# A transformer layer's matmul kernel: fixed order up to LayerNorm 1, one first group of two features, and the first half of gate and up in written order

## The chip, the core and the metric

The kernel runs on one core of a Trainium2 chip, as one launch. A core has engines that run side by side, each with its own queue of instructions: PE (TensorE, matmuls), ACT (ScalarE), DVE (VectorE), POOL (GpSimd) and SP (SyncE, which here issues most DMAs). They meet through semaphores. Matmuls read SBUF and write to PSUM banks. The metric is the time of one execution in device microseconds (us).

## The reference, cut to what matters

One layer over 256 latent tokens and 256 context tokens, D = 2048, all in fp32:

```python
sh1, sc1, g1, sh2, sc2, g2 = ada_mods(c, w_ada, b_ada)      # silu(c) @ w_ada + b_ada, six parts of D
csh1, csc1, *_ = ada_mods(c_ctx, w_ada, b_ada)
q, k, v of x   from modulate(x, sh1, sc1) @ w_in            # 2048 x 3072
q, k, v of ctx from modulate(ctx, csh1, csc1) @ w_in
heads = concat(window_sink_attention(...), global_attention(...))
x = layer_norm(ALPHA * x + g1 * (heads @ w_out))            # LayerNorm 1
u = modulate(x, sh2, sc2)
h = silu(u @ w_gate) * (u @ w_up)                           # 2048 x 5632 each
x = layer_norm(ALPHA * x + g2 * (h @ w_down))
```

## The kernel before

Each fp32 product is made as three products of rounded operands: a value is split into `hi` (rounded to fp32r, by a cast on ACT) and `lo` (the rest, by a subtraction on DVE), and a product of two values is hi·hi + lo·hi + hi·lo (`mm3`, L334 to L337: three matmuls of 128 x 128 by 128 x 512). Weights come in loads of 1 MB as a rule (`raw`, four buffers, L267), and are split in pieces of 1024 columns into `hi` and `lo` tiles (four buffers each, L268).

**Up to LayerNorm 1** the work is a list of steps with an engine, a length, what they wait for and which buffers they take and give (`Flow`, `F.add`). `F.run` (L229, called at L1522) plans an order when the kernel is built: it plays the steps forward with the given lengths, plays them backward for due times, and tries 1400 random changes of the ranks. Then it emits the steps in the best order found. PE also has 56 fill steps (`WARM`, L1354, the matmuls of L1343), which the plan may put wherever PE would wait. The input features of `x @ w_in` (16 blocks of 128) come in groups, `GROUPS` (L41): 1, 1, 2, 4 and 8 features. For each group the modulation is first made from columns of `w_ada` (L654, matmuls of the conditioning vector with loaded weights, or on DVE for the last four features), then `x` is flipped, modulated and split, and then multiplied with the group's rows of `w_in`, block by block. For the very first group the columns of `x` are loaded at once at L379 to L381.

All of this stands in a region (`tc.manual_schedule`, L369, with all five engines) in which each engine issues its instructions in the order in which the code emits them. The region goes on behind `F.run`, over the modulated operand of the next stage (`u2h`, `u2l`, L1676 to L1686), the first four products of gate and up, written out by hand, their copies to SBUF (L1715), and the normalisation of the other columns. It ends at L1719.

**The first half of gate and up** stands behind that end, so that its order is the scheduler's of the framework: it may take a later instruction of an engine ahead of an earlier one where data allow. It computes, for the first ten blocks `f` of 512 columns, the part of the sums over the first features: the first 4 of 16 feature blocks for `f` below 3, the first 8 for the others (`groups`, L1657), and for gate (`i` = 0) and up (`i` = 1). A step (L1664) is one load of weights for four feature blocks, with `project` (L1561): load on SP, then for each of two pieces a cast on ACT (L325) and a subtraction on DVE (L326), then 24 matmuls on PE. Where a sum has all its steps, its two row tiles are copied from PSUM to SBUF by ACT (`spill`, L1670):

```python
def step(g, f=f, i=i, w_=w_, st=st):
    if g == 0:
        st["accs"] = [acc_bank() for _ in range(NT)]
    project(st["accs"], w_, f, g, 0, groups[f] * 4 - 1)
    if g == groups[f] - 1:
        for t in range(NT):
            nc.scalar.copy(spills[f][i][:, t, :], st["accs"][t])
```

The list `first_half` holds these steps in order: two for f = 0 (made by hand ahead, so not run again), four for f = 1 and 2, and 28 for f = 3 to 9. Between them stand side sums: `scales` and `side` make the rest of the modulation from `w_ada` on DVE (L454, a load and two to four multiply-adds each), with a transpose and a sum on DVE (L1193, L1194), a fold on PE (L769) and small steps on DVE and POOL. `z_part(kk)` (L1538) makes two feature blocks of the operand: flips on PE (L1542), two activations and a cast on ACT (L1546, L1548), a subtraction on DVE (L1549).

**The second half** of gate and up (L1774) is again a region with all engines in written order; there a sum's ACT and DVE work is written two and more steps later than its last product. Then comes `w_down`, under the scheduler, and a tail on DVE and ACT.

Of the kernel before, what the change touches and what calls it, by code (L numbers as in the profile page):

```python
# [23 lines left out]
P = 128  # L24
# [16 lines left out]
GROUPS = ((0, 1), (1, 1), (2, 2), (4, 4), (8, 8))  # L41
# [6 lines left out]
WARM = 56  # L48
VECTOR_K = (12,)
EARLY_WARM = 5  # L50
COLD = 3
SEED = 4
# [13 lines left out]
SEED_G = 3  # L66
# [3 lines left out]
GET_NS = 1300  # L70

# [11 lines left out]
class Flow:  # L83

    ENGINES = ("SP", "PE", "ACT", "DVE", "POOL")
    SAME = {"SP": 0, "PE": 0, "ACT": 120, "DVE": 80, "POOL": 80}
    OTHER = {"SP": 2000, "PE": 270, "ACT": 180, "DVE": 160, "POOL": 150}  # L90
    AGAIN = 1300
    ROUNDS = 8
    TRIES = 1400
    DRAWS = 4
    LATE = {"SP": 1000.0, "ACT": 100.0, "DVE": 100.0}

    def __init__(self, room, begin):
        self.room, self.begin, self.steps, self.at = dict(room), begin, [], 0.0

    def add(self, eng, ns, fn, after=(), take=(), give=(), at=None, since=0.0):  # L100
        s = Step()
        s.since = since
        s.eng, s.ns, s.fn, s.take, s.give = eng, ns, fn, take, give
        s.after = [a if isinstance(a, tuple) else (a, 0) for a in after if a is not None]
        s.rank = (self.at if at is None else at, len(self.steps))
        for b in give:
            b.left += 1
        self.steps.append(s)
        return s

    def lag(self, a, b):
        return (self.SAME if a.eng == b.eng else self.OTHER)[a.eng]

    def forward(self):

        room, free, back, order, now = dict(self.room), dict(self.begin), [], [], 0.0
        later, ready = ({e: [] for e in self.ENGINES} for _ in range(2))
        left = {b: b.left for s in self.steps for b in s.give}
        for s in self.steps:
            s.next, s.left, s.when = [], len(s.after), s.since  # L120
        for s in self.steps:
            for a, early in s.after:
                a.next.append((s, early))
            if not s.left:
                heapq.heappush(later[s.eng], (s.when, s.rank, s))
        while len(order) < len(self.steps):
            while back and back[0][0] <= now:
                room[heapq.heappop(back)[1]] += 1
            moved = False
            for e in self.ENGINES:  # L130
                while later[e] and later[e][0][0] <= now:
                    heapq.heappush(ready[e], heapq.heappop(later[e])[1:])
                if free[e] > now:
                    continue
                for item in sorted(ready[e]):
                    s = item[1]
                    pools = [next((p for p in b.pools if room[p] > 0), None) for b in s.take]
                    if None in pools or any(room[p] < pools.count(p) for p in pools):
                        continue
                    ready[e].remove(item)  # L140
                    heapq.heapify(ready[e])
                    for b, p in zip(s.take, pools):
                        b.pool = p
                        room[p] -= 1
                    s.start, free[e] = now, now + s.ns
                    for b in s.give:
                        left[b] -= 1
                        if left[b] == 0:
                            lag = self.AGAIN if b.loaded else self.OTHER[e]
                            heapq.heappush(back, (free[e] + lag, b.pool))  # L150
                    for n, early in s.next:
                        n.left -= 1
                        n.when = max(n.when, free[e] - early + self.lag(s, n))
                        if n.left == 0:
                            heapq.heappush(later[n.eng], (n.when, n.rank, n))
                    order.append(s)
                    moved = True
                    break
            if not moved:
                times = [free[e] for e in self.ENGINES if free[e] > now and (ready[e] or later[e])]  # L160
                times += [later[e][0][0] for e in self.ENGINES if later[e] and later[e][0][0] > now]
                times += [back[0][0]] if back else []
                if not times:
                    return None, None
                now = min(times)
        return order, max(s.start + s.ns for s in self.steps)

    def backward(self, end):

        free = {e: end for e in self.ENGINES}  # L170
        later, ready = ({e: [] for e in self.ENGINES} for _ in range(2))
        left, by, start, now = {s: len(s.next) for s in self.steps}, {s: end for s in self.steps}, {}, end
        for s in self.steps:
            if not left[s]:
                heapq.heappush(later[s.eng], (-end, -(s.start + s.ns), s.rank, s))
        while len(start) < len(self.steps):
            moved = False
            for e in self.ENGINES:
                while later[e] and -later[e][0][0] >= now:
                    heapq.heappush(ready[e], heapq.heappop(later[e])[1:])  # L180
                if free[e] < now or not ready[e]:
                    continue
                s = heapq.heappop(ready[e])[-1]
                start[s] = free[e] = now - s.ns
                moved = True
                for a, early in s.after:
                    left[a] -= 1
                    by[a] = min(by[a], start[s] + early - self.lag(a, s))
                    if left[a] == 0:
                        heapq.heappush(later[a.eng], (-by[a], -(a.start + a.ns), a.rank, a))  # L190
            if not moved:
                times = [free[e] for e in self.ENGINES if free[e] < now and (ready[e] or later[e])]
                now = max(times + [-later[e][0][0] for e in self.ENGINES if later[e] and -later[e][0][0] < now])
        return start

    def replay(self, order, draw):

        free, rooms, end, late = dict(self.begin), {p: [0.0] * n for p, n in self.room.items()}, {}, {}
        left = {b: b.left for s in self.steps for b in s.give}
        for s, pools in order:  # L200
            t = max(free[s.eng], s.since, *(end[a] - early + self.lag(a, s) for a, early in s.after), 0.0)
            for b, p in zip(s.take, pools):
                t = max(t, heapq.heappop(rooms[p]))
                b.pool = p
            free[s.eng] = t + s.ns
            end[s] = free[s.eng] + draw.random() * (self.LATE.get(s.eng, 0.0) if s.ns else 0.0)
            for b in s.give:
                left[b] -= 1
                late[b] = max(late.get(b, 0.0), end[s] + (self.AGAIN if b.loaded else self.OTHER[s.eng]))
                if left[b] == 0:  # L210
                    heapq.heappush(rooms[b.pool], late[b])
        return max(end.values())

    def plan(self):
        order, last = self.forward()
        if not order:
            return False
        order = [(s, [b.pool for b in s.take]) for s in order]
        end = sum(self.replay(order, random.Random(i)) for i in range(self.DRAWS)) / self.DRAWS
        if end > self.end:  # L220
            return False
        self.end, self.last, self.rank, self.best = end, last, [s.rank[0] for s in self.steps], order
        return True

    def give_ranks(self, ranks):
        for i, (s, r) in enumerate(zip(self.steps, ranks)):
            s.rank = (r, i)

    def run(self):  # L229
        self.best, self.end = None, math.inf  # L230
        for _ in range(self.ROUNDS):
            self.plan()
            order, last = self.forward()
            if not order:
                break
            late = self.backward(last)
            self.give_ranks([late[s] for s in self.steps])
        assert self.best, "no step can start"
        draw = random.Random(SEED)
        for _ in range(self.TRIES):  # L240
            ranks = list(self.rank)
# [10 lines left out]
        for s, pools in self.best:  # L252
            for b, b.pool in zip(s.take, pools):
                pass
# [1718 lines left out]
```

## Time and profile before

| | us |
|---|---|
| median of 3 runs | 1124.76 (1124.49 to 1125.29) |
| profiled execution, span | 1124.1 |
| PE busy in it | 1103.7 |
| DVE busy | 905.7 |
| ACT busy | 603.6 |
| first product of `w_in` starts at | 16.4 |
| first half of gate and up, from its first product | 388.8 to 583.5 |
| last matmul starts at | 1111.6 |

A line of a timeline gives start, length, engine, line of the kernel, operation, the tiles (out<-in), shapes, a count, and in brackets the idle time of the engine before it with what ended it. A line of the view by window gives the stretch, its length, then busy time and instructions of PE, PEld (weight load), DVE, ACT and POOL, the granted clock of PE (1.00 is full), the DMA share and GB/s; asked for one line of code, it gives PE and PEld alone. A line of the view of waits says who waited for whom: us in total, times, longest. A line of the chain gives start, length and what ran. Matmul rows last longer than their distance (0.39 us against 0.23), since they are pipelined.

### The profile page before, as it was taken

What the parts mean: (1) busy time and instruction counts of PE and PEld (TensorE: products, weight loads), DVE (VectorE), ACT (ScalarE), POOL (GpSimd) and SP (SyncE); (2) the same over time, 40 slices, a digit from 0 to 9 for tenths busy, and PEclk for the clock granted to TensorE, in tenths of its full rate; (3) what the DMA queues carried; (4) which work ended last, traced back from release to release, by engine and by line L of the source; (5) the groups of instructions that cost most, each with busy time, mean ns of one, the idle gap of its engine ahead of it and who ended that gap; (6) DMA issues with size and microseconds to landing.
All of it is one profiled execution on the core that took longest, in us unless ns stands there. A gap on an engine that the chain in (4) does not pass through costs nothing.

```text
span 1124.1 us, 14152 instructions
## 1 busy us (share of the span) xinstructions
PE 1103.7 (98%) x5241; PEld 893.4 (79%) x5241; DVE 905.7 (81%) x1097; ACT 603.6 (54%) x879; POOL 47.1 (4%) x86
## 2 busy tenths in 40 slices
PE   8999999999999999999999999999999999999995
PEld 7677788788888778888888888888888788888884
DVE  3758999999989988787756876887875899678886
ACT  3335584787684355544464555655554565345541
POOL 1000050101200011000000000000000000000000
PEclk9999999999999999999999999999999999999998
DMA  9999999697999879989858798998896576546651
GB/s 298 388 391 373 390 366 370 225 312 215 356 311 375 303 284 341 326 309 340 295 189 297 264 340 273 314 308 302 311 321 222 159 253 223 190 149 231 225 217 75
DMA packets 179452, 321.27 MB, mean 286 GB/s; under 512 B 8979, under 2 KB 51379, under 8 KB 177077
## 3 DMA queue, kind: packets, MB, share of 16 engines
q1 hardware_dynamic: 177350, 319.23, 81.1%
q10 hardware_dynamic: 1808, 1.11, 0.3%
q8 instruction: 41, 0.67, 0.2%
q14 instruction: 29, 0.24, 0.1%
q0 software_dynamic: 224, 0.02, 0.0%
HBM read 304.07 MB, written 16.25 MB: 285 GB/s over the span
## 4 chain that ended last, share of the span: by engine, by line
PE 94%; DVE 3%; DMA 2%; issue 0%; ACT 0%; DVEq 0%; ACTq 0%
PE acc L335 22%; PE acc L336 22%; PE acc L337 22%; PE wk L337 7%; PE wk L336 7%; PE wk L335 7%; PE wk L1130 2%; PE wk L654 2%; PE wk L1343 1%; DMA raw<-in_w_in_dram 1%; PE wk L822 1%; DMA raw<-in_w_ada_dram 1%; DMA adav<-in_b_ada_dram 1%; DVE adav L454 0%; DVE lo L332 0%
## 5 line engine op out<-in xcount | busy, mean ns | idle before, releaser
L326 DVE TENSOR_TENSOR lo<-raw,hi 128x1024 fp32r<-128x1024 f32 x232 | 280.5, 1221 | 126.4 <-ACT hi L325 124.7
L325 ACT CAST hi<-raw 128x1024 fp32r<-128x1024 f32 x232 | 243.3, 1055 | 241.3 <-PE acc L337 130.7
L337 PE MATMUL acc<-hi,u2l 128*128 128x512 f32 x448 | 174.6, 390 | 1.4 <-DVE u2l L1686 1.4
L336 PE MATMUL acc<-lo,u2h 128*128 128x512 f32 x448 | 174.9, 390 | 0.0
L335 PE MATMUL acc<-hi,u2h 128*128 128x512 f32 x448 | 174.7, 391 | 0.0
L603 ACT CAST hi<-raw 128x1024 fp32r<-128x1024 f32 (+1 forms) x86 | 87.5, 1031 | 92.0 <-DMA raw<-in_w_in_dram 40.1
L454 DVE SCALAR_TENSOR_TENSOR adav<-raw,cs,adav 128x1024 f32<-128x1024 f32 (+1 forms) x96 | 114.3, 1191 | 6.1 <-DMA raw<-in_w_ada_dram 2.5
L606 DVE TENSOR_TENSOR lo<-raw,hi 128x1024 fp32r<-128x1024 f32 (+1 forms) x86 | 101.8, 1197 | 21.5 <-ACT hi L603 21.5
L335 PE MATMUL acc<-hi,uh 128*128 128x512 f32 x256 | 103.5, 404 | 0.2 <-DVE qacc L889 0.2
L335 PE MATMUL acc<-hi,hTh 128*128 128x512 f32 x264 | 102.7, 389 | 0.6 <-ACT hi L331 0.6
L336 PE MATMUL acc<-lo,hTh 128*128 128x512 f32 x264 | 102.7, 389 | 0.0
L337 PE MATMUL acc<-hi,hTl 128*128 128x512 f32 x264 | 102.5, 389 | 0.0
L337 PE MATMUL acc<-hi,ul 128*128 128x512 f32 x256 | 100.2, 391 | 0.0
L336 PE MATMUL acc<-lo,uh 128*128 128x512 f32 x256 | 99.9, 390 | 0.0
L337 PE MATMUL wk<-hi,u2l 128*128 128x512 f32 x256 | 99.6, 389 | 0.0
L336 PE MATMUL wk<-lo,u2h 128*128 128x512 f32 x256 | 99.6, 389 | 0.0
L335 PE MATMUL wk<-hi,u2h 128*128 128x512 f32 x256 | 99.6, 389 | 0.0
L337 PEld LDWEIGHTS acc<-hi,u2l 128*128 128x128 f32 x448 | 84.1, 188 | 19.3 <-DVE u2l L1686 2.0
L336 PEld LDWEIGHTS acc<-lo,u2h 128*128 128x128 f32 x448 | 84.1, 188 | 18.9 <-DVE lo L326 1.5
L335 PEld LDWEIGHTS acc<-hi,u2h 128*128 128x128 f32 x448 | 84.0, 188 | 18.3 <-ACT u2h L1685 1.0
L335 PEld LDWEIGHTS acc<-hi,uh 128*128 128x128 f32 x256 | 48.2, 188 | 16.1 <-issue 3.8
L335 PEld LDWEIGHTS acc<-hi,hTh 128*128 128x128 f32 x264 | 49.5, 188 | 11.3 <-ACT hi L331 1.0
(296 smaller groups left out, 1765.0 us busy)
## 6 DMA issues: line engine op xcount, KB each, us to landing
raw<-in_w_ada_dram SPq DMA_DIRECT2D x63, 1024.0 KB, 7.2
raw<-in_w_up_dram SPq DMA_DIRECT2D x44, 1024.0 KB, 6.7
raw<-in_w_gate_dram SPq DMA_DIRECT2D x44, 1024.0 KB, 6.5
raw<-in_w_down_dram SPq DMA_DIRECT2D x44, 1024.0 KB, 5.3
raw<-in_w_ada_dram SPq DMA_DIRECT2D x66, 512.0 KB, 6.3
raw<-in_w_in_dram SPq DMA_DIRECT2D x18, 1024.0 KB, 7.6
raw<-in_w_out_dram SPq DMA_DIRECT2D x16, 1024.0 KB, 7.6
pd<-hx SPq DMA_DIRECT2D x64, 128.0 KB, 3.7
```

The source lines that it names most:

```text
L325: nc.scalar.copy(hi[:, :n], raw[:, s : s + n])
L326: nc.vector.tensor_tensor(lo[:, :n], raw[:, s : s + n], hi[:, :n].bitcast(F32), op=ALU.subtract)
L335: nc.tensor.matmul(ps, lhsT=xh, rhs=w[0], start=first, stop=False, skip_group_check=seeded)
L336: nc.tensor.matmul(ps, lhsT=xh, rhs=w[1], start=False, stop=False, skip_group_check=seeded)
L337: nc.tensor.matmul(ps, lhsT=xl, rhs=w[0], start=False, stop=last, skip_group_check=seeded)
L454: nc.vector.scalar_tensor_tensor(a[:, c : c + piece], raw[:, f : f + piece], cs[:, 4 * (g * (G4 * NB // w) + j) + 2, None], a[:, c : c + p ...
L603: nc.scalar.copy(hl.hi[:, :n], raw.t[:, s : s + n])
L606: nc.vector.tensor_tensor(hl.lo[:, :n], raw.t[:, s : s + n], hl.hi[:, :n].bitcast(F32), op=ALU.subtract)
L654: nc.tensor.matmul(bank.t[32 * j : 32 * j + 32, :width], lhsT=cs[:, 4 * k + 2 - 2 * i : 4 * k + 34 - 2 * i], rhs=raw.t[:, c * width : (c + ...
L822: nc.tensor.transpose(ps.t[:, (j * 2 + t) * P : (j * 2 + t + 1) * P], src, ident)
L1130: nc.tensor.matmul(o_ps.t[:, : 2 * P].rearrange("p (g q) -> p g q", q=32), lhsT=v, rhs=pv[:, k], start=k == 0, stop=k == 3)
L1343: nc.tensor.matmul(wps, lhsT=ident, rhs=ident, start=True, stop=True)
```

## The change

Four things change.

1. `Flow` no longer plans. The order of the steps up to LayerNorm 1 is a list of step numbers in the file (`PLAN`, 1245 numbers); a letter behind a number says which pool of buffers a load takes, and `w6` stands for six fill matmuls. The list has `w6`, `w3`, `w7` and `w12`, all of them ahead of step 63, the first product.
2. The first two features are one group: `GROUPS` begins with (0, 2). Their columns of `w_ada` are loaded as four loads of 1 MB, 256 columns wide, for shift and scale and two halves of the rows; those of feature 0 were one load of 1 MB and two of half a MB, 128 columns wide. `x` and `cx` are loaded 256 columns wide at the start.
3. The region is left only behind the whole first half of gate and up, so that all of it is issued as written.
4. The first step of f = 3 (`first_half[6]`) is emitted ahead of `z_part(4)` and `z_part(6)`, no longer behind them.

```diff
-GROUPS = ((0, 1), (1, 1), (2, 2), (4, 4), (8, 8))
+GROUPS = ((0, 2), (2, 2), (4, 4), (8, 8))
...
-WARM = 56
-COLD = 3
-SEED = 4
-SEED_G = 3
+SEED_G = 2
...
+PLAN = """
+4r 2r 1195 6a w6 3 5 0 w3 7 19 8a 946 w7 9 60r 10 1 61 14 11 1192 67r 49r 155a 27a 85r 13 12 15 16 17 20 50 68 21 22
+62 18 51 w12 63 64 69 52 56 86 38 23 65 66 87 70 55 74 72 76 37 89 59 28r 78r 79 80 31r 30r 116 137r 1193 73 77 29 71
...
+"""
...
-    def forward(self):
...
-    def backward(self, end):
...
-    def plan(self):
...
-    def run(self):
...
+    def run(self, order, warm):
+
+        left = {b: b.left for s in self.steps for b in s.give}
+        for word in order.split():
+            if word[0] == "w":
+                warm(int(word[1:]))
+                continue
+            s = self.steps[int(word.rstrip("abr"))]
+            assert not s.done and all(a.done for a in s.after)
+            for b in s.take:
+                b.pool = next((p for p in b.pools if len(b.pools) == 1 or p[0] == word[-1]))
+                self.room[b.pool] -= 1
+                assert self.room[b.pool] >= 0
+            s.fn()
+            s.done = True
...
-    first_cx = xt[:, :, D - P :]
-    nc.scalar.dma_start(xt[:, :, :P], x[:, :P].rearrange("(t p) d -> p t d", p=P))
-    nc.scalar.dma_start(first_cx, cx[:, :P].rearrange("(t p) d -> p t d", p=P))
+    first_cx = xt[:, :, D - 2 * P :]
+    nc.scalar.dma_start(xt[:, :, : 2 * P], x[:, : 2 * P].rearrange("(t p) d -> p t d", p=P))
+    nc.scalar.dma_start(first_cx, cx[:, : 2 * P].rearrange("(t p) d -> p t d", p=P))
...
+            if not c0 and not g:
+                for k in range(0, KD, nk):
+                    for i in range(2):
+                        r, ld = flow_load(w_ada, k, nk, i * D, width)
+                        last_load[:] = [ld]
+                        prev = F.add("PE", ns1, lambda i=i, r=r, k=k: fn(0, i, r, 0, nk, k), [ld, prev],
+                                     [] if prev else [bank], [r])
             if not c0:
-                for i, k, m, since in ((0, 0, KD, 7200.0), (1, 0, KD // 2, 9700.0), (1, KD // 2, KD // 2, 11300.0)):
-                    r, ld = flow_load(w_ada, k, m, i * D, width, ("raw",) if m == KD else ("b4",))
...
                 continue
...
-    F.run()
+    F.run(PLAN, warm)
...
-    region.__exit__(None, None, None)
     run(first_half[2:3])
     run(merge(first_half[3 : 2 * ONE_F], scales))
     combine(1)
+    run(first_half[2 * ONE_F : 2 * ONE_F + 1])
     z_part(4)
     z_part(6)
     cutoff = len(first_half) - 2
-    run(merge(first_half[2 * ONE_F : cutoff], side))
+    run(merge(first_half[2 * ONE_F + 1 : cutoff], side))
     for kk in range(EARLY_G * 4, KD, 2):
         z_part(kk)
     run(first_half[cutoff:])
+    region.__exit__(None, None, None)
```

More of the change, by code (lines that the diff above doesn't have):

```diff
@@ L1 @@
-import heapq
-import random
 import math
@@ L83, with __init__ @@
 class Flow:
[L88 to L98, printed above, removed]
+    def __init__(self, room):
+        self.room, self.steps, self.at = dict(room), [], 0.0
     def add(self, eng, ns, fn, after=(), take=(), give=(), at=None, since=0.0):
         s = Step()
[L102 to L105, printed above, removed]
+        s.eng, s.ns, s.fn, s.take, s.give, s.done = eng, ns, fn, take, give, False
+        s.after = [a[0] if isinstance(a, tuple) else a for a in after if a is not None]
         for b in give:
@@ L109, in add @@
         return s
-    def lag(self, a, b):
-        return (self.SAME if a.eng == b.eng else self.OTHER)[a.eng]
-    def forward(self):
-        room, free, back, order, now = dict(self.room), dict(self.begin), [], [], 0.0
-        later, ready = ({e: [] for e in self.ENGINES} for _ in range(2))
-        left = {b: b.left for s in self.steps for b in s.give}
[L119 to L166, printed above, removed]
@@ L168, in backward @@
-    def backward(self, end):
[L170 to L206, printed above, removed]
+    def run(self, order, warm):
+        left = {b: b.left for s in self.steps for b in s.give}
+        for word in order.split():
[10 more added lines that the diff above has]
+            s.done = True
@@ L207, in replay @@
             for b in s.give:
                 left[b] -= 1
-                late[b] = max(late.get(b, 0.0), end[s] + (self.AGAIN if b.loaded else self.OTHER[s.eng]))
                 if left[b] == 0:
-                    heapq.heappush(rooms[b.pool], late[b])
-        return max(end.values())
-    def plan(self):
[L215 to L223, printed above, removed]
@@ L225, in give_ranks @@
-    def give_ranks(self, ranks):
-        for i, (s, r) in enumerate(zip(self.steps, ranks)):
-            s.rank = (r, i)
-    def run(self):
[L230 to L241, printed above, removed]
-            a, w, d = draw.uniform(0, self.last), draw.uniform(2e3, 4e4), draw.gauss(0, 3e3)
-            near = [i for i, r in enumerate(ranks) if a <= r <= a + w]
-            kind, e = draw.random(), draw.choice(self.ENGINES)
-            for i in near:
-                if kind < 0.6:
-                    ranks[i] += draw.gauss(0, 3e3) if draw.random() < 0.3 else 0
-                else:
-                    ranks[i] += d if self.steps[i].eng == e else 0
-            self.give_ranks(ranks)
-            self.plan()
-        for s, pools in self.best:
-            for b, b.pool in zip(s.take, pools):
-                pass
-            s.fn()
@@ L258, in dit_layer @@
+                    self.room[b.pool] += 1
+        assert all(s.done for s in self.steps)
 @with_exitstack
@@ L539, in dit_layer @@
     fill(pa, 448)
-    F = Flow({"raw": RAW_BUFS, "araw": ADA_BUFS, "hl": HL_BUFS, "acc": 4, "wk": 4, "b4": NB4, "t2k": T2K},
-             {"SP": 1300.0, "PE": 7300.0, "ACT": 5000.0, "DVE": 4000.0, "POOL": 4000.0})
+    F = Flow({"raw": RAW_BUFS, "araw": ADA_BUFS, "hl": HL_BUFS, "acc": 4, "wk": 4, "b4": NB4, "t2k": T2K})
     pools = {"raw": wraw, "araw": araw}
@@ L648, in fn @@
         def fn(g, i, raw, k0, k1, base=0):
-            if g == i == k0 == 0:
+            if g == i == k0 == base == 0:
                 bank.t = wk_bank()
@@ L662, in flow_columns @@
             ns1 = nk / 4 * (40 + 1.67 * width)
-            if not c0:
-                for i, k, m, since in ((0, 0, KD, 7200.0), (1, 0, KD // 2, 9700.0), (1, KD // 2, KD // 2, 11300.0)):
-                    r, ld = flow_load(w_ada, k, m, i * D, width, ("raw",) if m == KD else ("b4",))
-                    last_load[:] = [ld]
-                    prev = F.add("PE", ns1 * m / KD + (60 if i else 440), lambda i=i, r=r, k=k, m=m: fn(k // nk, i, r, 0, m, k), [ld, prev],
-                                 [] if i else [bank], [r], since=since)
+            if not c0 and not g:
[5 more added lines that the diff above has]
+                                     [] if prev else [bank], [r])
+            if not c0:
                 continue
@@ L1338, in flow_out, with warm @@
             finish(t)
-    def warm(wps, n):
+    warm_room = []
+    def warm(n):
+        if not warm_room:
+            warm_room.append(acc_bank())
         for _ in range(n):
-            nc.tensor.matmul(wps, lhsT=ident, rhs=ident, start=True, stop=True)
+            nc.tensor.matmul(warm_room[0][:, :P], lhsT=ident, rhs=ident, start=True, stop=True)
     nc.vector.tensor_copy(identb, ident)
-    wps = Buf("wk")
-    def warm_step(i):
-        if i == 0:
-            wps.t = wk_bank()[:, :P]
-        warm(wps.t, 1)
-    warms = [None]
-    for i in range(WARM):
-        warms.append(F.add("PE", 430 if i < COLD else 225, lambda i=i: warm_step(i), [warms[-1]], [wps] if i == 0 else [], [wps], at=1e6))
     flow_inputs(0, (0.0, 0.0))
-    T = 18.0
+    T = 9.0
     last = len(GROUPS) - 1
@@ L1367, in dit_layer @@
         dur = 10.9 * n + 4.0 * GROUPS[g + 1][1]
-        if g == 0:
-            bs = (8.0, 9.0)
-        elif n == 1:
-            bs = (T, T + dur)
-        else:
-            weight = [2, 1, 2, 1, 1, 1]
-            bs = {b: T + dur * sum(weight[:i]) / 8 for i, b in enumerate(BLOCKS)}
-        span = (T + 0.1 * dur, T + 0.9 * dur) if g else (10.0, 20.0)
+        weight = [2, 1, 2, 1, 1, 1]
+        bs = {b: T + dur * sum(weight[:i]) / 8 for i, b in enumerate(BLOCKS)}
+        span = (T + 0.1 * dur, T + 0.9 * dur) if g else (T + 0.35 * dur, T + 0.75 * dur)
         flow_inputs(g + 1, span)
@@ L1378, in dit_layer @@
         T += dur
-    start.after = [(last_load[0], 0)]
-    start.left = 1
+    start.after = [last_load[0]]
     gate_from = T
@@ L1472, in dit_layer @@
         raw, ld = flow_load(w_ada, g * 4, 4, 3 * D + NB, NB)
-        ld.after, ld.left = [(m0_sum, 2400)], 1
+        ld.after = [m0_sum]
         F.at = END + 45
```

11 lines of the change are left out of this document (added), and 32 rows, old and new, of the table PLAN.

## The prediction

> **What bounds the kernel now.** I read the page first: the busy times, then the chain that ended last.
>
> ```profile
> span 1124.1 us, 14152 instructions
> PE 1103.7 (98%) x5241; PEld 893.4 (79%) x5241; DVE 905.7 (81%) x1097; ACT 603.6 (54%) x879; POOL 47.1 (4%) x86
> PE 94%; DVE 3%; DMA 2%; issue 0%; ACT 0%; DVEq 0%; ACTq 0%
> ```
>
> TensorE is busy 98% of the span and is 94% of the chain. So any new wait that stops PE is paid in full, and little is there to be won: the 20 us in which PE is not busy, and fill matmuls. The profiled execution spans 1124.1 us; the median of the timed runs is 1124.76 us, so 0.7 us lies around the span, and I add to the median.
>
> Next comes the stage that leaves the scheduler's hands: the first half of the gate and up blocks. The window view (time and length, then busy PE, PEld, DVE, ACT, POOL, then granted clock and DMA):
>
> ```profile
> 388.80:569.60 180.80, 178.65 (x814) 145.61 (x811) 140.29 (x151) 90.52 (x115) 12.49 (x21) 1.00 0.88 311
> 569.60:583.50 13.90, 13.90 (x71) 11.75 (x70) 7.79 (x9) 11.83 (x20) 0.00 (x0) 1.00 0.42 149
> ```
>
> PE idles 2.15 us in 195 us, though ACT works only half of it. Why it never waits is in the view of waits of that stretch, and in ACT's timeline at its beginning:
>
> ```profile
> ACT hi L325 <- PE acc L337: 40.1, 27, 2.7
> PE acc L337 <- DVE u2l L1686: 1.4, 1, 1.4
> PE wk L1510 <- DVE xt L1278: 0.5, 1, 0.5
> ```
> ```profile
> 399.84 1.06 ACT L325 CAST hi<-raw 128x1024 fp32r<-128x1024 f32 x1 [2.73 <-PE acc L337]
> 401.21 1.07 ACT L1715 COPY spill<-acc 128x512 f32<-128x512 f32 x2 [0.32 <-PE acc L337]
> 402.17 2.01 ACT L325 CAST hi<-raw 128x1024 fp32r<-128x1024 f32 x2
> ...
> 404.55 1.06 ACT L325 CAST hi<-raw 128x1024 fp32r<-128x1024 f32 x1
> 408.69 1.27 ACT L1670 COPY spill<-acc 128x512 f32<-128x512 f32 x2 [3.08 <-PE acc L337]
> ```
>
> A step needs two casts (two pieces of its weights). By 405.6 four have run, so those of the step after the one then on PE are done before that one's sums are copied out (L1670) at 408.69. Casts wait 27 times for PE to return a weight buffer: they run as far ahead as four buffers allow. But the code writes a step as load, two casts, two subtractions, 24 products and, where its sum ends, two copies of the sums (L1664, L1670). The casts before the copies are the scheduler's doing.
>
> **Change 1, the region is held open over the first half.** ACT must then issue as written: both copies of a finished sum, which wait for PE's last product, and behind them the next step's casts. DVE's subtraction waits for the cast, PE for both. Nothing else is in PE's queue, which goes in written order too. The price of one such boundary, from rows of the trace (a last product and its copies, a run copy-copy-cast, a cast with its subtraction, and three starts in a row of products):
>
> ```profile
> 408.94 0.39 PE L337 MATMUL acc<-hi,u2l 128*128 128x512 f32 x1
> ```
> ```profile
> 437.81 1.27 ACT L1670 COPY spill<-acc 128x512 f32<-128x512 f32 x2 [3.70 <-PE acc L337]
> 438.97 2.00 ACT L325 CAST hi<-raw 128x1024 fp32r<-128x1024 f32 x2
> ```
> ```profile
> 35.77 1.05 ACT L603 CAST hi<-raw 128x1024 fp32r<-128x1024 f32 x1 [0.53 <-DMA raw<-in_w_in_dram]
> ...
> 36.85 1.23 DVE L606 TENSOR_TENSOR lo<-raw,hi 128x1024 fp32r<-128x1024 f32 x1 [1.12 <-ACT hi L603]
> ```
> ```profile
> 443.73 0.39 PE L335 MATMUL acc<-hi,u2h 128*128 128x512 f32 x1
> ...
> 444.41 0.39 PE L335 MATMUL acc<-hi,u2h 128*128 128x512 f32 x1
> ```
>
> Count from the start of the sum's last product. The first copy starts 0.25 us earlier (408.69 against 408.94; it needs the other row tile only). The cast follows 1.16 us behind it (438.97 - 437.81), at +0.91, and ends at +1.97. One product (cast part only) can go; the second needs the subtraction, done at +1.97 + 0.03 + 1.23 = +3.23. Products run 0.227 us apart (0.68 for three), so the second would have gone at +0.45. **Lost: 2.8 us.** The second piece is ready before the first is used up. Ends: 2.5 if waits overlap better, 3.4 if the first copy too waits for the last product.
>
> How many? The sums that end in copies are one row of the view by tile:
>
> ```profile
> L1670 ACT COPY spill<-acc x36: 576/587/592, 408.7 to 583.1; 128x512 f32<-128x512 f32 x36
> ```
>
> 36 copies are 18 sums of two. Behind each comes a boundary, and one more behind the four hand-written copies (L1715) ahead of them: 19. One holds the four z parts (below); **18 x 2.8 = 50.4 us**, ends 45 and 61.
>
> The z parts (flips on PE, four activations and casts on ACT) cost nothing now, covered by prefetched products. These rows price them: the first two of four on ACT, and PE's share of two:
>
> ```profile
> 570.90 1.47 ACT L1546 ACTIVATE uf<-wk,mB,mA 128x256 f32<-128x256 f32 x3
> ...
> 574.18 1.04 ACT L1546 ACTIVATE uf<-wk,mB,mA 128x256 f32<-128x256 f32 x2
> ```
> ```profile
> 570.36 1.75 PE wk L1542 x16
> ```
>
> One is 1.64 us of ACT (3.28 for two), some 1.45 without the cast overlap, and 0.88 of PE. Parts 4 and 6 stand between two steps of one sum: flips end one at +1.1, ACT starts at about +1.3 and is through at +4.4, then cast and subtraction, second product at +6.7; less the 0.45 at which it would have gone and the 1.75 of flips, **4.5 us**. The four late ones stand in the last-but-one boundary: ACT from +1.3 for 5.7 us, cast at +7.0, subtraction done at +9.3; less 0.45 and 3.5 us of flips, **5.4 us**. Together 9.9, ends 7 and 13. Moving one step ahead of parts 4 and 6 only chooses which wait covers which.
>
> What goes away is the 1.4 us wait for u2l. DVE had three side sums put ahead of it, which waited for a DMA:
>
> ```profile
> 395.82 2.33 DVE L454 SCALAR_TENSOR_TENSOR adav<-raw,cs,adav 128x512 f32<-128x512 f32 x3 [2.18 <-DMA adav<-in_b_ada_dram]
> ```
>
> As written, they come behind it. **-1.5 us** with the small wait for a fold. The 0.5 us stays; it is hand order already.
>
> **Change 2, first two features as one group, and a fixed order.** The rows: DMA of the first 20 us, the fill matmuls by stretch, the sums of one feature (128 wide, half of them) and of two (256 wide, half), feature 0's last sum and the first product, and a wait of feature 1.
>
> ```profile
> 0.00:10.00 10.00, 5.86 (x49) 5.15 (x50) 1.08 (x4) 1.92 (x4) 3.33 (x8) 1.00 0.87 231
> 10.00:20.00 10.00, 10.00 (x88) 8.39 (x87) 4.68 (x9) 5.83 (x11) 0.00 (x0) 1.00 1.11 344
> ```
> ```profile
> 20.00:44.00 24.00, 1.93 (x12) 1.65 (x12) 1.00 1.09 359
> 44.00:100.00 56.00, 3.25 (x24) 2.99 (x24) 1.00 1.04 392
> 100.00:130.00 30.00, 4.71 (x36) 4.32 (x36) 1.00 1.04 381
> ```
> ```profile
> 6.88 1.94 PE wk L654 x32
> ...
> 41.09 1.86 PE wk L654 x32
> ```
> ```profile
> 12.48 0.64 PE L654 MATMUL wk<-raw,cs 128*32 128x128 f32 x16
> ...
> 16.42 0.48 PE L335 MATMUL acc<-hi,uh 128*128 128x512 f32 x1
> ```
> ```profile
> PE wk L688 <- ACT ada L683: 1.1, 1, 1.1
> ```
>
> Two features cost 4 x 1.94 = 7.8 us of PE now and 2 x 1.86 = 3.7 as one group: -4. The first product then needs four loads of 1.05 MB, half a MB of inputs and one of weights, 5.3 MB, where the windows moved 2.3 MB by 10 us and 344 GB/s after: 18.7 us, and 3.3 us from last sum to first product (16.42 - 13.12): 22 instead of 16.4, +5.6. Fill behind the first product is 9.9 us now. In the new list every fill word stands ahead of the first product; but DMA is full to 130 us, so waits will stand in for more than half of that fill: -3.4 of 9.9. Its 28 fills only cover the wait for the loads. Feature 1's wait for its column sums goes too (1.1 us), and its flips and sums fall into the wait ahead of the first product: -3 for both, an estimate. **Sum -5 us**; ends -11 (all later fill goes) and +3 (none does, and the first product is 3 us later still).
>
> **Sum:** 1124.8 - 5 - 1.5 + 50.4 + 9.9 = 1178.6.
>
> **The clock.** Once PE stops, the granted clock falls; the only place that shows it is the tail (last product, then clock by window):
>
> ```profile
> 1111.56 0.39 PE L337 MATMUL acc<-hilo,hTl 128*128 128x512 f32 x1
> ```
> ```profile
> 1114.00:1114.50 0.50, 0.00 (x0) 0.00 (x0) 0.43 (x3) 0.00 (x0) 0.00 (x0) 0.83 0.00 0
> 1114.50:1115.00 0.50, 0.00 (x0) 0.00 (x0) 0.46 (x4) 0.00 (x0) 0.00 (x0) 0.50 0.00 0
> ```
>
> 0.83 over half a us is full speed until 1114.33: 2.4 us after the last product's end. A boundary idles PE 1.8 us, then 1.0 us, with one product between: just short. The two z places idle it for 3 to 4 us in one piece: there I expect the half clock, for about as long as PE stood, 1.5 us lost each: **+3**, ends 0 and 8. **Forecast 1181.6 us.** The Trainium skill ("TensorE: Matmul & The Clock Gate", section "The HAM clock gate") says that the clock halves after an idle window of about 3.4 us and comes back after a busy one; by it the boundaries would add nothing, and by an estimate from it a z place would lose 1.7 us. The trace's 2.4 us is shorter than that window, so the rule's safety isn't shown here.
>
> **Rivals.**
> *The half clock at many boundaries.* For it: 2.4 us of idle sufficed once, and a boundary loses 2.8. Against: the 1.4 us wait for u2l left the clock of the stage's window at 1.00. If all 18 fell and each lost 1.6 us: +29, 1211. Chance 12%.
> *DVE is late.* Side sums (L454, 1.3 us each) now stand between subtractions; where their load lands late, the next subtraction waits behind them. DVE is 78% busy in the stage (140.29 of 180.80), but new PE waits give it time. Half a us at 16 side steps and two folds: 1190. Chance 7%.
> *Not slower: casts stay ahead of copies.* If the region doesn't hold ACT to the written order at L1670, the change doesn't do what it says, each boundary is free, and z parts are covered: 1124.8 - 5 - 1.5 = 1118. The place is the first cast behind the copies of the second step; it decides as soon as two casts stand ahead of each pair. Against it: the second half, already held, has ACT as written, seeds of the next sum between casts:
>
> ```profile
> 604.82 1.05 ACT L325 CAST hi<-raw 128x1024 fp32r<-128x1024 f32 x1 [1.67 <-PE wk L337]
> 605.77 1.10 ACT L1760 COPY acc<-spill 128x512 f32<-128x512 f32 x2
> ```
>
> Chance 13%. At 2% something between leaves the time as it is.
>
> **How the numbers follow.** Forecast 66%, half clock 12%, DVE late 7%, not held 13%, unchanged 2%. Low end: 1124.8 - 1.5 + 45 + 7 - 11 = 1164; high end: up to the half clock, 1211. This leaves out the not-held case and little else. Slower by over 0.2% (about what a measurement of this kernel can tell) 85%, within 0.2% 2%, faster 13%.
>
> **What would show it.** Right: in the stage, 18 pairs of copies, each followed at once by a cast, PE idle behind each some 1.8 us for ACT and 1.0 us for DVE; PE busy share down to 93 or 94%; the stage some 59 us longer; from the second half on, everything as before, only later. Wrong: casts ahead of copies, PE dense at 0.227 us a product, or a first product far from 22 us.

## The result, and the profile after

The changed kernel takes 1204.77 us (median; 1200.3 to 1208.9), the one before 1125.03 us: 1.071 times as long (95% interval 1.068 to 1.074). The forecast was 1181.6 us, in a range of 1164 to 1211. The page of its profiled execution, the slowest of its four (1208.9 us):

```profile
span 1207.1 us, 13855 instructions
PE 1134.6 (94%) x5121; PEld 905.5 (75%) x5121; DVE 895.3 (74%) x1075; ACT 599.7 (50%) x874; POOL 41.5 (3%) x86
PE   8999999999999778888877999999999999999995
PEclk9999999999999887989898999999999999999998
```

PE's busy share falls from 98% to 94%, and the 40 slices show where: slices 14 to 22 lose busy time, and the granted clock falls in the same stretch. By the starts of the first products of each stage, the first half of gate and up begins at 384.2 us (388.8 before) and lasts 281.3 us, up to the first product of the second half. Before, it lasted 194.1 us, up to 582.9; the 583.5 of the table above lies three products into the second half. From there to the last matmul it is 528.8 us against 528.7. So 4.6 us were won at the start, 87.2 us lost in the stage, and nothing changed behind it.

The stage by window and by waits (columns as before):

```profile
384.18:665.48 281.30, 228.51 (x880) 175.96 (x877) 147.27 (x158) 98.60 (x131) 12.09 (x20) 0.88 0.60 207
```
```profile
PE acc L240 <- ACT hi L230: 37.1, 19, 6.2
PE acc L241 <- DVE lo L231: 15.7, 20, 1.9
```

Before, PE hardly waited there, and the clock was 1.00. Now it waits 19 times for a cast and 20 times for a subtraction, and 0.88 is the mean of full and half speed: a quarter of the stage runs at half. One boundary, ACT first, then PE (the last three products of a sum and the first two of the next), then DVE:

```profile
460.38 1.26 ACT L1563 COPY spill<-acc 128x512 f32<-128x512 f32 x2 [7.63 <-PE acc L242]
461.54 3.89 ACT L230 CAST hi<-raw 128x1024 fp32r<-128x1024 f32 x4
```
```profile
460.18 0.39 PE L240 MATMUL acc<-hi,u2h 128*128 128x512 f32 x1
460.40 0.39 PE L241 MATMUL acc<-lo,u2h 128*128 128x512 f32 x1
460.63 0.39 PE L242 MATMUL acc<-hi,u2l 128*128 128x512 f32 x1
462.64 0.50 PE L240 MATMUL acc<-hi,u2h 128*128 128x512 f32 x1 [1.62 <-ACT hi L230]
463.90 0.50 PE L241 MATMUL acc<-lo,u2h 128*128 128x512 f32 x1 [0.76 <-DVE lo L231]
```
```profile
462.62 2.36 DVE L231 TENSOR_TENSOR lo<-raw,hi 128x1024 fp32r<-128x1024 f32 x2 [5.90 <-ACT hi L230]
```

ACT sat idle for 7.63 us with the next casts behind the copies in its queue. From the sum's last product (460.63) the first product of the next comes at +2.01 and the second at +3.27, where the prediction's count had +2.0 and +3.25.

### The profile page after: what moved, and what is told of

Its sections match the earlier page's. It is cut to its first block, busy times and chain, and to the rows that moved or that the text cites. A ratio compares the mean times of both kernels' runs of the same rounds, so it can differ in the third digit from the quotient of the medians.

```text
span 1207.1 us, 13855 instructions
## 1 busy us (share of the span) xinstructions
PE 1134.6 (94%) x5121; PEld 905.5 (75%) x5121; DVE 895.3 (74%) x1075; ACT 599.7 (50%) x874; POOL 41.5 (3%) x86
## 5 line engine op out<-in xcount | busy, mean ns | idle before, releaser
L231 DVE TENSOR_TENSOR lo<-raw,hi 128x1024 fp32r<-128x1024 f32 x232 | 279.0, 1221 | 192.0 <-ACT hi L230 190.3
L230 ACT CAST hi<-raw 128x1024 fp32r<-128x1024 f32 x232 | 239.6, 1052 | 196.7 <-PE acc L242 91.0
L240 PE MATMUL acc<-hi,u2h 128*128 128x512 f32 x448 | 188.3, 420 | 37.1 <-ACT hi L230 37.1
L241 PE MATMUL acc<-lo,u2h 128*128 128x512 f32 x448 | 188.5, 421 | 15.7 <-DVE lo L231 15.7
L242 PE MATMUL acc<-hi,u2l 128*128 128x512 f32 x448 | 184.8, 413 | 0.0
L240 PEld LDWEIGHTS acc<-hi,u2h 128*128 128x128 f32 x448 | 90.3, 201 | 63.9 <-ACT hi L230 43.7
L241 PEld LDWEIGHTS acc<-lo,u2h 128*128 128x128 f32 x448 | 91.1, 203 | 42.0 <-DVE lo L231 22.9
L507 ACT CAST hi<-raw 128x1024 fp32r<-128x1024 f32 x84 | 87.8, 1052 | 55.1 <-PE acc L242 33.9
L510 DVE TENSOR_TENSOR lo<-raw,hi 128x1024 fp32r<-128x1024 f32 x84 | 101.3, 1221 | 9.4 <-ACT hi L507 9.2
L242 PEld LDWEIGHTS acc<-hi,u2l 128*128 128x128 f32 x448 | 91.1, 203 | 19.7 <-DVE u2l L1579 0.5
L1563 ACT COPY spill<-acc 128x512 f32<-128x512 f32 x36 | 21.1, 586 | 160.1 <-PE acc L242 158.4
```

Of the source, the lines that this page charges most:

```text
L230: nc.scalar.copy(hi[:, :n], raw[:, s : s + n])
L231: nc.vector.tensor_tensor(lo[:, :n], raw[:, s : s + n], hi[:, :n].bitcast(F32), op=ALU.subtract)
L240: nc.tensor.matmul(ps, lhsT=xh, rhs=w[0], start=first, stop=False, skip_group_check=seeded)
L241: nc.tensor.matmul(ps, lhsT=xh, rhs=w[1], start=False, stop=False, skip_group_check=seeded)
L242: nc.tensor.matmul(ps, lhsT=xl, rhs=w[0], start=False, stop=last, skip_group_check=seeded)
L507: nc.scalar.copy(hl.hi[:, :n], raw.t[:, s : s + n])
```

## The experiments

**Theory:** the loss is ACT's queue, copies that wait for PE ahead of the next casts, and the half clock that these waits bring. **Rivals:** written order as such (side sums and folds), the fixed list, or a clock that falls for another cause.

**The fixed list and the first group alone.**

```diff
     for n in range(1, 4):
         for t in range(NT):
             normalise(n, t)
+    region.__exit__(None, None, None)
     run(first_half[2:3])
...
-    run(first_half[2 * ONE_F : 2 * ONE_F + 1])
...
-    run(merge(first_half[2 * ONE_F + 1 : cutoff], side))
+    run(merge(first_half[2 * ONE_F : cutoff], side))
...
-    region.__exit__(None, None, None)
```

> The changed kernel with the region ended where it ended before, and the step of f = 3 back behind z parts 4 and 6: the fixed list and the first group of two features alone. Theory (the start gains a little, the held first half costs all the rest): the first half of gate and up begins 4.6 us earlier (384.2 instead of 388.8, as in the changed kernel) and is as dense as before: 1120 us. Rival (the fixed list costs something by itself, later on): 1125 us or more.

Measured: 1119.11 us (1118.4 to 1120.7), ratio 0.995 (0.994 to 0.997). The fixed list costs nothing; this part of the change alone beats the kernel before. The stage by window:

```profile
386.60:577.41 190.81, 190.66 (x880) 157.27 (x877) 147.10 (x158) 101.21 (x131) 10.30 (x20) 1.00 0.87 303
```

It begins 2.2 us earlier here and is 3.2 us shorter than before, with no PE wait left in it. So only part of the gain lies at the start: the rest is the waits of 1.4, 0.5 and 0.2 us of before and the slow products behind them, which the scheduler's order for this stage happens not to have. The stage's begin differs between the profiles of kernels with this same start, from 383.0 to 387.5 us.

**The region alone.** The kernel before, with the end of the region moved:

```diff
-    region.__exit__(None, None, None)
     run(first_half[2:3])
...
     run(first_half[cutoff:])
+    region.__exit__(None, None, None)
```

> The kernel before with the region held open over the first half, and nothing else changed. Theory: all of the loss is there; the stage is some 87 us longer, as in the changed kernel, and without the start's gain: 1205 to 1214 us, with PE waits of some 37 us for casts and 16 us for subtractions and the clock at half speed in many windows. Rival (the loss comes from the fixed list and the region together): under 1185 us.

Measured: 1199.71 us (1197.8 to 1203.1), ratio 1.067 (1.065 to 1.069). The loss is the region's; the expected range was missed below by 5 us. The clock fell less often, 0.94 over the stage instead of 0.88, and the step of f = 3 isn't moved here, so PE waits 18 times for a cast, once less. The two parts, -5.5 and +75.1 us, add up to 69.6, where the whole change cost 79.7: the move (2.7 us, below) is in neither part, and the stage has half clock in 19 windows of 3.41 us in the profile of the whole change and in 10 here.

```profile
389.20:654.69 265.49, 214.36 (x880) 165.32 (x877) 147.71 (x159) 99.59 (x134) 11.45 (x21) 0.94 0.63 221
```

Two copies in a stretch at full clock give the price of a boundary without the clock:

```profile
473.12 1.26 ACT L1670 COPY spill<-acc 128x512 f32<-128x512 f32 x2 [8.77 <-PE acc L337]
474.28 3.90 ACT L325 CAST hi<-raw 128x1024 fp32r<-128x1024 f32 x4
486.95 1.26 ACT L1670 COPY spill<-acc 128x512 f32<-128x512 f32 x2 [8.77 <-PE acc L337]
```

13.83 us for a sum of 48 products at 0.227 us (10.88): 2.95 us, of which 2.8 are the wait and the rest the first products after it, which follow more slowly.

**Casts ahead of copies, still in written order.** The changed kernel, with each pair of copies held back until the next step's casts are written:

```diff
+    copies = []
...
         w = load_split(w_, g * 4, f * NB)
+        while copies:
+            copies.pop(0)()
...
-                        nc.scalar.copy(spills[f][i][:, t, :], st["accs"][t])
+                        copies.append(lambda t=t, accs=st["accs"]: nc.scalar.copy(spills[f][i][:, t, :], accs[t]))
...
-            nc.scalar.copy(spills[0][i][:, t, :], firsts[i][t])
+            copies.append(lambda i=i, t=t: nc.scalar.copy(spills[0][i][:, t, :], firsts[i][t]))
```

> The changed kernel with each pair of copies of a finished sum written behind the casts of the next step; all is still held in written order. Theory (ACT's queue: copies that wait for PE stand ahead of casts): the 18 boundaries vanish and the clock with them; what stays are the two places with z parts, 10 us of waits and some 3 us of half clock: 1129 to 1133 us. Rival (written order as such, above all side sums between DVE's subtractions and folds in PE's queue): over 1170 us, with PE still waiting at most sums.

Measured: 1136.51 us (1136.3 to 1138.4), ratio 1.011 (1.009 to 1.012). All is in written order here too, and 68 us are back: the place of the copies decides, not the order as such. The expected time was missed by 4 us; the two places with z parts each took two windows of half clock, 6.8 us, and the clock over the stage is 0.97. PE's waits:

```profile
PE acc L240 <- ACT hi L230: 10.1, 2, 6.2
PE acc L241 <- DVE lo L231: 2.9, 4, 1.6
```

The two waits for casts are the places with z parts. ACT at the first of them shows the queue, z work and then the casts that PE waits for:

```profile
428.34 1.01 ACT L1439 ACTIVATE uf<-wk,mB,mA 128x256 f32<-128x256 f32 x2
429.39 0.62 ACT L1441 CAST u2h<-uf 128x512 fp32r<-128x512 f32 x1
429.91 3.88 ACT L230 CAST hi<-raw 128x1024 fp32r<-128x1024 f32 x4
```

The four waits for subtractions are two behind those casts, and two behind side sums on DVE. That rival is real and small: all four waits together are 2.9 us.

**Six fill matmuls at each boundary.** The waits stay; PE is kept busy in them:

```diff
+    fills = {(u, f, 0): 6 for f in range(1, SPLIT_F) for u in (False, True)}
+    fills[False, 0, 1] = 6
+    fills[False, ONE_F, 1] = 16
+    fills[True, SPLIT_F - 1, 0] = 26
...
         w = load_split(w_, g * 4, f * NB)
+        if fills.get((w_ is w_up, f, g)):
+            bank = wk_bank()
+            for _ in range(fills[w_ is w_up, f, g]):
+                nc.tensor.matmul(bank[:, :P], lhsT=ident, rhs=ident, start=True, stop=True)
```

> The changed kernel with six fill matmuls (1.4 us) in PE's queue at each boundary, 16 and 26 at the two places with z parts; PE waits as long as before for what it needs, but each window of 3.4 us keeps PE busy for more than half. Theory (the half clock follows from the waits, by windows of 3.4 us that are idle for more than half): clock 1.00 throughout, all of the half-speed cost gone, the waits stay: 1179 us. Rival (the half clock has another cause, or wants a gap free of any wait): still 1200 to 1209 us.

Measured: 1184.00 us (1183.1 to 1184.8), ratio 1.053 (1.051 to 1.055), 21 us less than the changed kernel, and its runs agree within 2 us where those of the changed kernel differ by 9.

```profile
385.47:640.26 254.79, 234.44 (x1180) 191.94 (x1177) 147.07 (x158) 98.70 (x131) 12.11 (x20) 1.00 0.66 229
```

The clock stays at 1.00, and the stage is 26.5 us shorter than in the changed kernel's profile. From one pair of copies to the next it is 13.83 us for a sum of 48 products here too, so the fills left the waits of these boundaries as they were. The 87.2 us of that profile split into 60.7 us of waits (254.8 - 194.1) and 26.5 us of half clock. That profile is the slowest run of its kernel; by the medians the half clock cost 20.8 us.

**Two fills instead of six**, to see when the clock falls:

```diff
-    fills = {(u, f, 0): 6 for f in range(1, SPLIT_F) for u in (False, True)}
-    fills[False, 0, 1] = 6
+    fills = {(u, f, 0): 2 for f in range(1, SPLIT_F) for u in (False, True)}
+    fills[False, 0, 1] = 2
```

> The changed kernel with two fill matmuls (0.45 us) at each boundary instead of six; 16 and 26 at the two places with z parts. Theory (the clock is set at the end of each window of 3.41 us on a fixed grid, to half where PE was idle for more than some 1.63 us of it): a boundary leaves at most some 1.9 us idle in one window, so some boundaries fall and others don't, by where they lie on the grid: 3 to 8 spells of half clock, 1186 to 1196 us, and no window with under 1.6 us idle loses the clock. Rival (only a gap in one piece counts): at most 1.3 us in one piece, no spell at all, 1180 us.

Measured: 1194.19 us (1192.8 and 1195.6), ratio 1.061 (1.059 to 1.063), six spells of half clock in the stage. Some boundaries fall and others don't, as expected, and it isn't the length of one piece that decides. The section at the end has the windows; two with just under 1.6 us idle fell too, so the limit isn't sharp there.

**Casts ahead of the z parts as well**, on top of casts ahead of copies:

```diff
+    def split_ahead(w_, f, g):
+        ahead[w_ is w_up, f, g] = load_split(w_, g * 4, f * NB)
+        while copies:
+            copies.pop(0)()
...
-        w = load_split(w_, g * 4, f * NB)
+        w = ahead.pop((w_ is w_up, f, g), None) or load_split(w_, g * 4, f * NB)
...
-    run(first_half[2 * ONE_F : 2 * ONE_F + 1])
+    split_ahead(w_gate, ONE_F, 0)
     z_part(4)
     z_part(6)
+    run(first_half[2 * ONE_F : 2 * ONE_F + 1])
...
+    split_ahead(w_up, SPLIT_F - 1, 0)
     for kk in range(EARLY_G * 4, KD, 2):
         z_part(kk)
```

> The kernel with casts ahead of copies, and at the two places with z parts the casts of the next step written ahead of them as well; the step of f = 3 is back behind parts 4 and 6, so that its products run beside their ACT work. Theory (what is left in that kernel is ACT's queue at the z parts): waits of 4.0 and 6.2 us for casts go, and with them both spells of half clock: 1120 to 1123 us. Rival (z parts cost PE their own chain of flip, activation, cast and subtraction): over 1128 us.

Measured: 1123.82 us (1121.4 to 1126.4), ratio 0.9985 (0.9975 to 0.9994), a little above what was expected. Of the waits for casts 0.7 us is left, of those for subtractions 2.7, and the stage has full clock and takes 195.5 us. Written order is now level with the scheduler of before, but not with the fixed list under the scheduler (1119.11).

**A whole step ahead.** Each step's casts and subtractions written behind those of the step before, ahead of that step's products, copies and side sums. The copies are held back as in the two kernels with casts first, and the step of f = 3 stands behind z parts 4 and 6:

```diff
+    keys = [(u, f, g) for f in range(1, SPLIT_F) for u in (False, True) for g in range(1 if f < ONE_F else EARLY_G)]
+    follow = dict(zip(keys, keys[1:]))
...
-        w = load_split(w_, g * 4, f * NB)
+        key = (w_ is w_up, f, g)
+        w = ahead.pop(key, None) or load_split(w_, g * 4, f * NB)
+        if key in follow:
+            u, nf, ng_ = follow[key]
+            ahead[u, nf, ng_] = load_split(w_up if u else w_gate, ng_ * 4, nf * NB)
+        while copies:
+            copies.pop(0)()
...
-    run(first_half[2 * ONE_F : 2 * ONE_F + 1])
     z_part(4)
     z_part(6)
+    run(first_half[2 * ONE_F : 2 * ONE_F + 1])
```

> All in written order, with each step's casts and subtractions written one whole step ahead: behind those of the step before, and ahead of that step's products, of its copies and of the side sums. Theory: what still stops PE with casts ahead of copies (subtractions behind side sums on DVE, some 3 us) goes too: 1118 to 1121 us, level with the fixed list alone under the scheduler (1119). Rival (four weight buffers don't carry casts a step ahead in a fixed order, or loads come late): 1125 us or more.

Measured: 1129.55 us (1128.3 to 1130.8), ratio 1.004 (1.003 to 1.005): missed, and worse than the step before. The waits for subtractions shrank from 2.7 us to 0.8, and a longer one came:

```profile
PE wk L675 <- DVE part L1100: 4.6, 1, 4.6
```

The side sums now stand behind the subtractions of one more step (2.4 us on DVE), which wait 1.9 us for casts, as these do for a weight buffer from PE. So the sum that the fold needs starts 4.4 us later than in the kernel before this one, counted from the begin of the stage, and the fold stands in PE's own written order, ahead of products of the next step. PE's wait also cost one window of half clock, from 421.3 us.

**The start without its fills.** The fixed list alone, with `w6`, `w3`, `w7` and `w12` taken out of `PLAN`:

> The fixed list alone under the scheduler, without its 28 fill matmuls at the start. Theory (the clock comes up at the end of the first window that is busy for more than half): it comes up some windows later, about 3.4 to 7 us into the products instead of 9 us ahead of them, and half of that time is lost: 1120.5 to 1123 us instead of 1119. Rival (fills only pass the time): 1119 us, unchanged.

Measured: 1118.76 us (1117.5 to 1119.3), ratio 0.994 (0.993 to 0.996), not to be told from 1119.11 with them. The time is the rival's, but the fills don't only pass the time. Without them PE was busy for 1.32 us of the window from 19.49 us, and the clock stood at half for the next window, among the first products (22.9 to 26.3 us); with them it stayed at 1.00 there. The first product came at 21.6 us instead of 24.6 in the two profiles, which would make up for it. But with the fills it came at 22.1 to 24.8 us in the profiles of the kernels with this list, so it isn't shown that the fills delay it.

**The step of f = 3 back behind the z parts**, in the kernel with six fills:

```diff
-    fills[False, ONE_F, 1] = 16
+    fills[False, ONE_F, 0] = 16
...
-    run(first_half[2 * ONE_F : 2 * ONE_F + 1])
     z_part(4)
     z_part(6)
...
-    run(merge(first_half[2 * ONE_F + 1 : cutoff], side))
+    run(merge(first_half[2 * ONE_F : cutoff], side))
```

> The kernel with six fills at each boundary, with the step of f = 3 back behind z parts 4 and 6 (16 fills stand at that place, as before, now ahead of that step). The prediction said of this move that it only chooses which wait covers which. Theory now (ACT's queue): with the move there are two waits, 2.8 us at the boundary ahead of the step and 4.5 us behind the z parts, and without it one of 4.5 us, in which the boundary is contained: 2.8 us less, 1181 us instead of 1184. Rival (as predicted): no change, 1184 us.

Measured: 1180.42 us (1179.8 to 1181.5) against 1184.00, ratio 1.049 (1.047 to 1.051), and the stage by window is 2.7 us shorter:

```profile
384.25:636.36 252.11, 232.64 (x1168) 190.56 (x1165) 147.07 (x158) 98.71 (x131) 10.23 (x20) 1.00 0.66 231
```

## Why the prediction was right, and where it was wrong

The direction, the place and the cause were right: ACT's written order, with PE waiting at each finished sum. The forecast itself is 23 us below the measured time. The range held the time only because its high end was the rival of the half clock, to which the prediction gave 12%. Its waits come out close, 58.8 us (50.4 + 9.9 - 1.5) against 60.7, and that is in part luck: one boundary too many (2.8 us) stands against z parts that were priced too low (2.3 us) and a wait on DVE that was put at nothing (2.0 us).

- **The boundary: right.** 2.8 us of wait as counted, 2.95 us with the slower first products. Undoing it alone (casts ahead of copies) gave 68 us back, with the half clock that it had brought.
- **The count: one too many.** Predicted were 18 plain boundaries, one with the four late z parts, and the place of z parts 4 and 6. The 19 waits for casts are 17, one and one. The boundary that is missing is the last, into the second half: its products follow without a gap. The region ends there, and three casts of the second half, which has a region of its own, ran ahead of the last copies. ACT (the third of these casts, the copies) and PE in the timeline of the changed kernel, on both sides of that end:

```profile
662.96 1.05 ACT L230 CAST hi<-raw 128x1024 fp32r<-128x1024 f32 x1 [1.67 <-PE acc L242]
665.00 1.27 ACT L1563 COPY spill<-acc 128x512 f32<-128x512 f32 x2 [0.99 <-PE acc L242]
```
```profile
665.26 0.39 PE L242 MATMUL acc<-hi,u2l 128*128 128x512 f32 x1
665.49 0.39 PE L240 MATMUL wk<-hi,u2h 128*128 128x512 f32 x1
```

- **The z parts: right in kind, short in size.** Counted 4.5 and 5.4 us; the starts of the last flip and of the two products behind it give 5.0 (4.17 + 1.26, less the 0.45 of two products without a wait) and 7.2 us (6.44 + 1.26 - 0.45). The mis-sized term is the share of PE that was taken off: the row `570.36 1.75 PE wk L1542 x16` was read as the flips of two parts, and it is those of four. In the changed kernel two parts have 8 flips and four have 16:

```profile
446.92 1.03 PE L1435 MATMUL wk<-ident,xt 128*128 128x128 f32 x8
451.86 0.80 PE L240 MATMUL acc<-hi,u2h 128*128 128x512 f32 x1 [3.90 <-ACT hi L230]
...
643.98 1.91 PE L1435 MATMUL wk<-ident,xt 128*128 128x128 f32 x16
652.05 0.80 PE L240 MATMUL acc<-hi,u2h 128*128 128x512 f32 x1 [6.17 <-ACT hi L230]
```

From the last product to the last flip it is 1.86 us at the late place, not 3.5, which is nearly all of the error there, and 1.00 us at the first, not 1.75, where ACT started sooner than counted (0.9 us behind the last product, not 1.3) and made up for part of it.

- **The move of a step: wrong.** "Only chooses which wait covers which" should have read: adds a boundary of its own, since the copies ahead of that step wait for PE, and the z parts wait again behind it. 2.7 us.
- **The start: right in sum, partly in the wrong place.** -5 against -4.6 in the changed kernel's profile and -5.5 for that part alone. The first product came at 23.4 us (predicted 22). But 3.2 of the 5.5 us of that part alone lie in the stage behind LayerNorm 1, and that stage's begin varies by 4.5 us between profiles with the same start, so the agreement with -4.6 from a single one is in part luck.
- **The rival "DVE is late": real, but at one place.** Of the 20 waits for subtractions 19 are those of the second product at a boundary or z place. The other stands behind side sums on DVE and costs 2.0 us (from 619.27, the start of the product before, to 621.54, less 0.23), where the rival had 18 such places:

```profile
621.54 0.50 PE L241 MATMUL acc<-lo,u2h 128*128 128x512 f32 x1 [1.88 <-DVE lo L231]
```

- **The u2l wait: right.** No such wait stands at that place in the held order.
- **The clock: the step that failed.** The prediction took the tail's 2.4 us as the least idle time in one piece, and said of a boundary's 1.8 and 1.0 us "just short". It expected +3 from the two z places; the half clock cost 26.5 us in the profiled run. The rival that gave +29 for all boundaries, with 12%, is nearly what happened: 14 of the 17 plain boundaries lost the clock, and so did both z places and the late subtraction. With the measured sizes the sum gives 1124.8 - 4.6 + 60.7 + 26.5 = 1207.4, beside the profiled run's 1208.9. How many boundaries fall isn't fixed by the change: in the region alone only some did, by where they lay on the clock's grid (last section).
- **The rival "not slower": excluded.** Each pair of copies but the last has the next step's casts right behind it, at the late z parts behind the z work.

## What to carry to other kernels

When an engine is put in written order, look for the instruction in its queue that waits for the engine it feeds, and for what stands behind it: a copy of finished sums ahead of the next operands' casts cost 3 us a time, and writing the casts first took it away. Each reordering should then be read for the next queue that it blocks, as the fold on PE did here. Waits of PE also have a second price in the clock, which here went by how much of a window they filled and not by how long each was; it was about a third of the loss and most of the spread between runs (9 us with it, 2 us with the six fills).

## What the runs showed of the hardware

The granted clock is set on a grid of 3.41 us: in the changed kernel each spell of half clock in the stage lasts 3.41 us or twice that, and each stretch between two of them a whole number of 3.41 us. It falls where PE was idle for about half of the window before. The tail of the kernel before shows it already when it is cut at the grid:

```profile
1110.92:1114.33 3.41, 1.03 (x5) 1.00 0.21 80
1114.34:1117.70 3.36, 0.00 (x0) 0.50 0.00 0
```

The window was busy for 1.03 us and still took the clock. In the region alone, two windows beside the ones that follow them, by PE, PEld, DVE, ACT and POOL:

```profile
515.90:519.31 3.41, 1.68 (x6) 1.20 (x7) 2.47 (x3) 3.41 (x4) 0.00 (x0) 1.00 0.01 3
519.32:522.71 3.39, 3.39 (x10) 2.61 (x9) 2.15 (x2) 0.33 (x1) 0.00 (x0) 0.50 0.71 198
...
529.55:532.96 3.41, 1.79 (x8) 1.14 (x7) 0.24 (x1) 2.38 (x4) 0.00 (x0) 1.00 0.00 0
532.97:536.37 3.40, 2.63 (x11) 1.99 (x11) 3.40 (x4) 2.57 (x3) 0.00 (x0) 1.00 0.11 14
```

1.68 us busy lost the clock (10 products in the next window, where 3.41 us at 0.227 us hold 15), 1.79 us kept it. With two fills the limit shows again, by PE alone, at another place:

```profile
436.99:440.40 3.41, 1.86 (x7) 1.00 0.02 5
440.41:443.81 3.40, 3.40 (x17) 1.00 0.73 230
512.08:515.49 3.41, 1.70 (x6) 1.00 0.63 237
515.50:518.90 3.40, 3.40 (x9) 0.50 0.69 209
426.75:430.16 3.41, 1.84 (x8) 1.00 0.26 100
430.17:433.57 3.40, 3.40 (x10) 0.50 0.66 199
```

Here 1.70 and 1.84 us lost the clock and 1.86 us kept it. So there is no sharp limit in these rows: 1.84 us lost it here, and 1.79 us kept it in the region alone. All that they show is that a window at full clock that was busy for up to 1.70 us lost it, and one busy for 1.86 us kept it.

Most spells last one window, in which PE is busy throughout. At each z place of the changed kernel, PE waited for part of the half-speed window too, and the spell lasted two:

```profile
451.46:454.87 3.41, 2.55 (x5) 0.50 0.00 0
454.87:458.28 3.41, 3.41 (x9) 0.50 0.83 262
```

2.55 us busy at half speed did not bring the clock back; 3.41 us did.

A boundary idles PE for some 2.4 us if it falls into one window and for a part of that in each if it is cut by the grid, so what the waits cost in clock goes by where the boundaries lie. The four runs of the changed kernel, 1200.3 to 1208.9 us, are 16 to 25 us above the median with six fills.

The Trainium skill ("TensorE: Matmul & The Clock Gate", section "The HAM clock gate") says that the window is 3413 ns long and runs freely, without starting anew with the kernel. These traces agree: the windows are 3.41 us long, and the grid lies differently in each run. The Trainium skill (the same section of "TensorE: Matmul & The Clock Gate") also says that the clock falls after an idle window. These rows show less to be enough: half a window, though the idle half lay in pieces of 1.8 us at most at a boundary.
